# A hybrid decoder layer in split fp32: seven more pairs of matrix blocks by seven products, and split buffers opened and closed in two parts

## The chip, the cores and the metric

The kernel runs on one core of a Trainium2 chip. It is fp32 throughout and its matrix products run on TensorE (PE); VectorE (DVE), ScalarE (ACT) and GpSimd (POOL) do the rest, and SyncE (SP) issues the loads of the weights. Each engine works through its own instructions in a fixed order and waits for the others by semaphores. The time is that of one execution on the device in microseconds, given as the median of several; less is better.

## What is computed

256 tokens of width 2048 go through one layer:

```python
u = rmsnorm(h, ln1_w)
lru_x, lru_g, q, k, v, ret_g = split(u @ w_in)          # 2048 -> 6 x 1024
y_lru = rg_lru(causal_conv4(lru_x)) * gelu(lru_g)
y_ret = group_norm(retention(rope(q), rope(k), v)) * silu(ret_g)
h = h + concat(y_lru, y_ret) @ w_out                    # 2048 -> 2048
u = rmsnorm(h, ln2_w)
h = h + (silu(u @ w_gate) * (u @ w_up)) @ w_down        # 2048 -> 5632 -> 2048
out = rmsnorm(h, final_norm_w)
```

All weights come from HBM once, some 240 MB. The change is in the part from `w_out` on.

## The kernel before

**Splitting.** A matrix product of fp32 accuracy is made of three TensorE products of rounded operands (type fp32r): each operand is split into a high part, the rounded copy, and a low part, the rest. The function `split` (L122) does it: ACT casts (L123: `wh`, `ah`, `sh`, `t4h`, `bh`) and DVE subtracts (L124: `wl`, `al`, `sl`, `t4l`, `bl`). `three` (L680) issues the three matmuls of 128x512: high by high (L683), low weight part (L684), low activation part (L685).

**Pairs and blocks.** From the output projection on, the work is cut into blocks, and a block into pairs: a pair is two 128-row slices of the weights by two 512-column halves, loaded in two transfers of 512 KB (`raw`), and it multiplies the 256 tokens. Blocks 0 and 1 are the output projection, 2 to 12 gate/up (called gate/up 0 to 10 here), each with 8 pairs; then come two down blocks with 22 pairs each. A block sums into four PSUM banks c11, c21, c12, c22. A plain pair takes eight products (24 matmuls; `EIGHT`). A summed pair takes seven (21 matmuls; `SEVEN`), by the Strassen-Winograd scheme: DVE first makes sums of the raw weights (L661, four 512-wide operations a pair) and of the activations (L561 to L564), and these sums are split as well.

**Shared products and the joint.** Of the seven products of a summed pair, four can be done in a block ahead (`Block.share`, L795). They go into the four banks of the coming block while the block before is still at work. When the last of them is done, the banks are rewritten, called the joint here: ACT copies c11 to p1 (L806), DVE makes p = c12 − p1 (L807) and q = p − c22 (L808), ACT copies q to c12 (L809), and DVE makes c22 = q − c21 (L810) and c21 = c21 − p (L811). Only then may the block add its own products to c12, c22 and c21: three for each summed pair (`direct`, L813) and eight for each plain one (`plain`, L817). Down's second block has its summed pairs whole, with no shared part.

**What sets the order.** For each block a string in `STEPS` says what comes after what: `p` a plain pair, `h` half of one, `s` a shared product set for the next block, `d` the direct products of an own summed pair. `SUMMED` lists the summed pairs of each block; for down it is `SUMMED_DOWN` and `ORDER_DOWN`, and `EARLY_DOWN` names the pairs of down's first block that are shared. Loads are issued three ahead of their use. From this program a scheduler makes each engine's order, so that an instruction whose inputs are expected late can move behind others.

**Buffers.** Raw loads have a pool of 6 tiles, splits one of 4 pairs (`wh` and `wl`), the rest 60 activation tiles. From block 3 to block 12 two more raw and two more split buffers are open (`swap` and `stop_more`, L1097 to L1104), in the space that the early stages left. Ahead of down, `swap_back` (L1106) closes them and opens the rows' and weights' pools: the eight kept rows of the residual are loaded back (L1112, POOL's queue) and the four pieces of the final norm's weights `fw` (L893, POOL's queue). In down's second block DVE multiplies finished rows by `fw` (L984).

## Time and profile before

| | before |
|---|---|
| median of 3 runs | 1083.56 us (1082.75 to 1084.05) |
| the profiled execution | 1082.46 us, span 1080.7 us |
| mean granted TensorE clock | 0.998 |
| TensorE busy | 1070.2 us, 99% of the span |
| VectorE busy | 964.1 us, 89% |
| ScalarE busy | 664.5 us, 61% |
| a gate/up block | 41.6 us |

A gate/up block's time is that from one joint to the next between 484.64 and 776.02 us of the span, seven blocks. The span is counted from the first instruction to the last; the execution's own time is a little longer. The chain of waits goes back from the last instruction to what released each; a row of the timeline has its start, its length, engine, line and operation.

### The profile page before, as it was taken

To read this page: it belongs to the slowest core of one execution; us is meant where nothing else is said; L and a number is where in the kernel's file an instruction comes from. 1 tells how busy PE (TensorE), PEld (TensorE's weight loads), DVE (VectorE), ACT (ScalarE), POOL (GpSimd) and SP (SyncE) were. 2 spreads that over 40 slices of the span, in tenths; PEclk is the share of its full clock that TensorE was granted. 3 is DMA by queue.
4 is the path that set the end of the run, shared out by engine and by line. 5 is a ranking of instruction groups with operands and counts; after the bars stand their busy time and mean duration, and the time that the engine had idled before them with its cause. 6 is when DMAs were issued, how large, how long until landed. Compare 5 with 4: busy or idle time off the path is not lost.

```text
span 1080.7 us, 14590 instructions
## 1 busy us (share of the span) xinstructions
PE 1070.2 (99%) x5089; PEld 897.7 (83%) x5089; DVE 964.1 (89%) x1399; ACT 664.5 (61%) x947; POOL 57.2 (5%) x73
## 2 busy tenths in 40 slices
PE   9999999999999999999999999999999999999997
PEld 7888888888888888888888888888888888888886
DVE  7889789988878889989999999999999889997886
ACT  7666644468756676656656565665656656654563
POOL 0602230000000000000000000000002000000001
PEclk9999999999999999999999999999999999999999
DMA  9965475554556588677776777777767856474662
GB/s 325 336 213 171 159 254 166 183 176 158 192 195 234 183 304 273 231 235 256 257 270 228 251 260 242 263 269 232 258 234 270 289 181 214 162 245 159 214 212 101
DMA packets 71386, 244.62 MB, mean 226 GB/s; under 512 B 8208, under 2 KB 8592, under 8 KB 71312
## 3 DMA queue, kind: packets, MB, share of 16 engines
q1 hardware_dynamic: 68400, 236.34, 64.6%
q0 software_dynamic: 1472, 4.72, 1.3%
q10 hardware_dynamic: 1440, 2.62, 0.6%
q8 instruction: 40, 0.66, 0.2%
q14 instruction: 34, 0.28, 0.1%
HBM read 239.46 MB, written 4.19 MB: 225 GB/s over the span
## 4 chain that ended last, share of the span: by engine, by line
PE 98%; DVE 1%; DMA 1%; POOL 0%; SPq 0%; ACT 0%; issue 0%; POOLq 0%; ACTq 0%
PE c L685 22%; PE c L683 22%; PE c L684 22%; PE fm L194 11%; PE fm L196 5%; PE tm L174 3%; PE tm L175 3%; PE tm L176 3%; PE p L683 1%; PE p L685 1%; PE p L684 1%; PE ft L865 1%; DMA x<-in_x 1%; PE ht L588 0%; PE sc L492 0%; DVE wl L124 0%
## 5 line engine op out<-in xcount | busy, mean ns | idle before, releaser
L123 ACT CAST wh<-raw 128x1024 fp32r<-128x1024 f32 (+1 forms) x498 | 462.9, 959 | 323.8 <-PE c L685 130.8
L124 DVE TENSOR_TENSOR wl<-raw,wh 128x1024 fp32r<-128x1024 f32 (+1 forms) x498 | 542.2, 1115 | 72.5 <-ACT wh L123 71.2
L684 PE MATMUL c<-wl,ah 128*128 128x512 f32 x826 | 322.7, 391 | 0.0
L685 PE MATMUL c<-wh,al 128*128 128x512 f32 x826 | 321.8, 390 | 0.0
L683 PE MATMUL c<-wh,ah 128*128 128x512 f32 x826 | 280.3, 391 | 0.0
L683 PEld LDWEIGHTS c<-wh,ah 128*128 128x128 f32 x826 | 155.1, 188 | 32.0 <-ACT wh L123 0.3
L685 PEld LDWEIGHTS c<-wh,al 128*128 128x128 f32 x826 | 155.2, 188 | 31.8
L684 PEld LDWEIGHTS c<-wl,ah 128*128 128x128 f32 x826 | 155.2, 188 | 31.6
L194 PE MATMUL fm<-u,wh 128*128 128x512 f32 x512 | 161.4, 396 | 0.0
L196 PEld LDWEIGHTS fm<-u,wl 128*128 128x128 f32 x512 | 96.1, 188 | 22.4
L196 PE MATMUL fm<-u,wl 128*128 128x256 f32 x512 | 101.2, 279 | 0.0
L661 DVE TENSOR_TENSOR raw<-raw,raw 128x512 f32<-128x512 f32 x114 | 78.4, 689 | 2.0
L661 DVE TENSOR_TENSOR raw<-raw 128x512 f32<-128x512 f32 x114 | 78.3, 688 | 1.4
L194 PEld LDWEIGHTS fm<-u,wh 128*128 128x128 f32 x512 | 78.4, 189 | 0.3
L684 PE MATMUL c<-wl,sh 128*128 128x512 f32 x192 | 74.3, 390 | 0.0
L685 PE MATMUL c<-wh,sl 128*128 128x512 f32 x192 | 73.7, 390 | 0.0
L683 PE MATMUL c<-wh,sh 128*128 128x512 f32 x192 | 67.3, 391 | 0.3 <-ACT sh L123 0.3
L176 PE MATMUL tm<-wh,u 128*128 128x512 f32 x128 | 48.7, 391 | 0.0
L175 PE MATMUL tm<-wl,u 128*128 128x512 f32 x128 | 48.7, 393 | 0.0
L174 PE MATMUL tm<-wh,u 128*128 128x512 f32 x128 | 46.9, 394 | 1.4 <-ACT u L298 1.4
L683 PEld LDWEIGHTS c<-wh,sh 128*128 128x128 f32 x192 | 36.1, 188 | 8.1 <-ACT sh L123 0.7
L685 PEld LDWEIGHTS c<-wh,sl 128*128 128x128 f32 x192 | 36.1, 188 | 7.5
(247 smaller groups left out, 1027.4 us busy)
## 6 DMA issues: line engine op xcount, KB each, us to landing
raw<-in_w_gu SPq DMA_DIRECT2D x216, 512.0 KB, 5.3
raw<-in_w_down SPq DMA_DIRECT2D x91, 512.0 KB, 4.6
raw<-in_w_out SPq DMA_DIRECT2D x34, 512.0 KB, 3.7
raw<-in_w_lx SPq DMA_DIRECT2D x16, 512.0 KB, 6.4
raw<-in_w_k SPq DMA_DIRECT2D x16, 512.0 KB, 3.6
raw<-in_w_q SPq DMA_DIRECT2D x16, 512.0 KB, 4.2
raw<-in_w_rg SPq DMA_DIRECT2D x16, 512.0 KB, 3.5
raw<-in_w_lg SPq DMA_DIRECT2D x16, 512.0 KB, 3.5
```

What stands on the lines that cost most here:

```text
L123: act.copy(out=dst_h, in_=src)
L124: v.tensor_tensor(out=dst_l, in0=src, in1=dst_h.bitcast(F32), op=ALU.subtract)
L174: pe.matmul(ps, ah, wh, start=first, stop=False)
L175: pe.matmul(ps, ah, wl, start=False, stop=False)
L176: pe.matmul(ps, al, wh, start=False, stop=last)
L194: pe.matmul(ps, wh, hl, start=n + i == 0, stop=False)
L196: pe.matmul(ps[:, :S], wl, hl[:, :S], start=False, stop=n + i == len(order) - 1)
L661: v.tensor_tensor(out=dst, in0=a, in1=b, op=ALU.add)
L683: pe.matmul(p, ah, bh, start=first, stop=False, skip_group_check=onto)
L684: pe.matmul(p, ah, bl, start=False, stop=False, skip_group_check=onto)
L685: pe.matmul(p, al, bh, start=False, stop=last, skip_group_check=onto)
L865: pe.transpose(pt[:, o : o + P], g[:, (2 * b + c) * P : (2 * b + c) * P + P], ident)
```

## The change

1. Five more summed pairs in blocks 1, 2, 3 and 12: block 1 goes from two to four, 2 from two to three, 3 and 12 from three to four. The `STEPS` strings of blocks 0 to 3, 11 and 12 change with them; since the strings are given for the coming block's shares, block 0 now has four `s`.
2. Down's second block sums nine pairs and not seven (12 and 19 are new) and takes its pairs in another order.
3. The extra buffers come in two parts. `split_near`, one split buffer, opens already ahead of block 0, and closes in down's second block. `split_far`, one split buffer, and `raw_far`, two raw ones, open ahead of block 3 in the space of the first residual rows and close in down's first block. At these steps (`hooks`) the kept rows come back four by four, and `fw` is loaded when the near part closes, behind step 8 of down's second block. The sums of the activations for pairs 12 and 19 have a pool of their own for a while (`sums`).
4. For the first two column blocks, DVE takes `fw` when the product is run and no longer when it is planned.

The core of the diff:

```diff
-SUMMED = ((), (4, 5), (2, 3), (1, 2, 3)) + ((0, 1, 2, 3),) * 8 + ((1, 2, 3),)
-SUMMED_OUT, SUMMED_FFN = (4, 5), (0, 1, 2, 3)
+SUMMED = ((), (4, 5, 6, 7), (1, 2, 3)) + ((0, 1, 2, 3),) * 10
+SUMMED_OUT, SUMMED_FFN = (4, 5, 6, 7), (0, 1, 2, 3)
...
-STEPS = ("pppspppspp", "ppspdpsdpp", "pdpsdpspspp", "pspsdpsdpsdp") + ("psdhsdhsdhsdhp",) * 7 + ("psdpsdpsddp", "psdpsdpsdpp")
+STEPS = ("ppspspspsppp", "psdpsdpsddp", "pspsdpsdpsdp") + ("psdhsdhsdhsdhp",) * 9 + ("psdpsdpsddp",)
...
-SUMMED_DOWN = (9, 12, 15, 17, 19), (5, 7, 9, 11, 13, 15, 17)
-ORDER_DOWN = (3, 4, 0, 5, 6, 1, 7, 8, 2) + tuple(range(9, 22)), tuple(range(22))
+SUMMED_DOWN = (9, 12, 15, 17, 19), (5, 7, 9, 11, 12, 13, 15, 17, 19)
+ORDER_DOWN = (3, 4, 0, 5, 6, 1, 7, 8, 2) + tuple(range(9, 22)), (0, 12, 1, 19, 2, 5, 3, 7, 4, 9, 6, 11, 8, 13, 10, 15, 14, 17, 16, 18, 20, 21)
+BESIDE = (12, 19)
...
     def split_tiles():
-        turn_of[1] += 1
-        pool_ = more[1] if more and turn_of[1] % 3 == 0 else wpool
-        return [pool_.tile([P, 1024], F32R, tag=g, name=nm(g)) for g in ("wh", "wl")]
+        counts[0] += 1
+        n = counts[0] % (4 + len(more_split))
+        p = more_split[n - 4] if n >= 4 else wpool
+        return [p.tile([P, 1024], F32R, tag=g, name=nm(g)) for g in ("wh", "wl")]
...
+            if i in hooks[ordered]:
+                program.append(([], hooks[ordered][i]))
...
-                defer(13 + 2 * cb + t, lambda: v.tensor_tensor(out=h, in0=h, in1=f, op=ALU.mult))
+                defer(13 + 2 * cb + t, lambda: v.tensor_tensor(out=h, in0=h, in1=fw[cb], op=ALU.mult))
...
+    def near_begins():
+
+        early.close()
+        more_split.append(near.enter_context(tc.tile_pool(name="split_near", bufs=1, reuse_waits="tile")))
...
+    def near_ends():
+        near.close()
+        late.append(ctx.enter_context(tc.tile_pool(name="late", bufs=4, reuse_waits="tile")))
+        load_fw()
+
+    def far_begins():
+
+        kept_stack.close()
+        more_split.append(
+            far.enter_context(tc.tile_pool(name="split_far", bufs=1, side="right", reuse_waits="tile"))
+        )
+        more_raw.append(
+            far.enter_context(tc.tile_pool(name="raw_far", bufs=2, side="right", reuse_waits="tile"))
+        )
...
+    def rows_back(d):
+        resid[0] = ctx.enter_context(tc.tile_pool(name=f"resid_{d}", bufs=4, side="right", reuse_waits="tile"))
+        for key in [(cb, t) for cb in (2 * d, 2 * d + 1) for t in range(2)]:
             htok[key] = res_tile("htok")
             pool.dma_start(out=htok[key], in_=kept[key])
...
+    hooks = {0: {6: far_stops, 9: far_ends}, 1: {5: near_stops, 8: near_ends, 7: sums_end}}
...
     for b, after in zip(blocks, blocks[1:] + [down]):
+        if b.index == 0:
+            program.append(([], near_begins))
         if b.index == 3:
-            program.append(([], swap))
-        if b.index == NB + 1:
-            program.append(([], stop_more))
+            program.append(([], far_begins))
         b.put(after)
-    program.append(([], swap_back))
```

Lines move by three to 29: L123 and L124 become L126 and L127, L661 L664, L683 to L685 L686 to L688, L806 to L811 L811 to L816, L893 L898, L984 L990, L1112 L1141.

**How instructions move, first place: DVE at the joint into gate/up 0.** In the rows c12_777 (before) and c12_793 (after) are banks of gate/up 0; p and q belong to its joint. Before:

```order
L807 TENSOR_TENSOR p_802_3940<-c12_777_3814,p1_801_3939 128x512
L124 TENSOR_TENSOR wl_806_3951<-raw_804_3948,wh_805_3950 128x1024
L124 TENSOR_TENSOR wl_809_3966<-raw_807_3963,wh_808_3965 128x1024
L808 TENSOR_TENSOR q_803_3941<-p_802_3940,c22_775_3806 128x512
L124 TENSOR_TENSOR wl_812_3972<-raw_810_3969,wh_811_3971 128x1024
L810 TENSOR_TENSOR c22_775_3806<-q_803_3941,c21_776_3810 128x512
L811 TENSOR_TENSOR c21_776_3810<-c21_776_3810,p_802_3940 128x512
```

After:

```order
L600 TENSOR_TENSOR htok_629_3132<-c21_679_3364,htok_629_3132 128x512
L127 TENSOR_TENSOR wl_842_4091<-raw_840_4088,wh_841_4090 128x512
L600 TENSOR_TENSOR htok_640_3190<-c12_680_3368,htok_640_3190 128x512
L600 TENSOR_TENSOR htok_652_3251<-c22_678_3360,htok_652_3251 128x512
L664 TENSOR_TENSOR raw_840_4088<-raw_840_4088 128x512
L812 TENSOR_TENSOR p_829_4044<-c12_793_3869,p1_828_4043 128x512
L127 TENSOR_TENSOR wl_836_4070<-raw_834_4067,wh_835_4069 128x1024
L664 TENSOR_TENSOR raw_840_4088<-raw_840_4088,raw_849_4144 128x512
L813 TENSOR_TENSOR q_830_4045<-p_829_4044,c22_791_3861 128x512
L664 TENSOR_TENSOR raw_849_4144<-raw_840_4088,raw_849_4144 128x512
L815 TENSOR_TENSOR c22_791_3861<-q_830_4045,c21_792_3865 128x512
L816 TENSOR_TENSOR c21_792_3865<-c21_792_3865,p_829_4044 128x512
```

Before, the residual rows of the second output block (L597) come behind the joint. Now their four additions (L600 after) stand ahead of it, together with the split wl_842, and two weight sums stand between the steps of the joint. On TensorE, 6 products and 16 transposes of 128x128 now lie between the last shared product of this joint and the first product on c22; before, 50 products.

**Second place: the joint into down's first block**, on TensorE. c12_1666 (before) and c12_1700 (after) are banks of down's first block, c11_1585 to c12_1588 and c22_1612 those of the last gate/up block. Before, the last shared product and its neighbours:

```order
L683 MATMUL c11_1585_7562<-wh_1706_8104,ah_841_4117 128x512
L683 MATMUL c12_1588_7574<-wh_1706_8104,ah_841_4117 128x512
L684 MATMUL c12_1666_7926<-wl_1696_8044,sh_1693_8039 128x512
L685 MATMUL c12_1666_7926<-wh_1695_8043,sl_1694_8040 128x512
L684 MATMUL c11_1585_7562<-wl_1707_8105,ah_841_4117 128x512
L685 MATMUL c11_1585_7562<-wh_1706_8104,al_842_4118 128x512
L684 MATMUL c12_1588_7574<-wl_1707_8105,ah_841_4117 128x512
L685 MATMUL c12_1588_7574<-wh_1706_8104,al_842_4118 128x512
```

After:

```order
L688 MATMUL c22_1698_8025<-wh_1732_8171,sl_1728_8147 128x512
L688 MATMUL c21_1699_8029<-wh_1732_8171,sl_1728_8147 128x512
L688 MATMUL c12_1700_8033<-wh_1729_8150,sl_1728_8147 128x512
L688 MATMUL c22_1612_7639<-wh_1743_8217,al_872_4223 128x512
L686 MATMUL c22_1612_7639<-wh_1749_8244,ah_871_4222 128x512
L687 MATMUL c22_1612_7639<-wl_1750_8245,ah_871_4222 128x512
L688 MATMUL c22_1612_7639<-wh_1749_8244,al_872_4223 128x512
L686 MATMUL c11_1697_8021<-wh_1754_8263,ah_1752_8259 128x512
L686 MATMUL c22_1698_8025<-wh_1754_8263,ah_1752_8259 128x512
L686 MATMUL c21_1699_8029<-wh_1754_8263,ah_1752_8259 128x512
L686 MATMUL c12_1700_8033<-wh_1754_8263,ah_1752_8259 128x512
L687 MATMUL c11_1697_8021<-wl_1755_8264,ah_1752_8259 128x512
```

Before, after the last shared product (the row c12_1666 with sl_1694) 45 products follow up to the first that adds to c12_1666 again. Now four products of the last gate/up block follow the last shared product (c12_1700 with sl_1728), and then down's own products begin on all four banks.

On DVE the same joint, before:

```order
L807 TENSOR_TENSOR p_1712_8127<-c12_1666_7926,p1_1711_8126 128x512
L124 TENSOR_TENSOR wl_1716_8138<-raw_1714_8135,wh_1715_8137 128x1024
L124 TENSOR_TENSOR wl_1719_8153<-raw_1717_8150,wh_1718_8152 128x1024
L808 TENSOR_TENSOR q_1713_8128<-p_1712_8127,c22_1664_7918 128x512
L124 TENSOR_TENSOR al_1722_8159<-ff_1011_4925,ah_1721_8158 128x512
L124 TENSOR_TENSOR wl_1724_8163<-raw_1720_8156,wh_1723_8162 128x1024
L124 TENSOR_TENSOR al_1730_8199<-ff_1090_5291,ah_1729_8198 128x512
L810 TENSOR_TENSOR c22_1664_7918<-q_1713_8128,c21_1665_7922 128x512
L811 TENSOR_TENSOR c21_1665_7922<-c21_1665_7922,p_1712_8127 128x512
```

After:

```order
L812 TENSOR_TENSOR p_1746_8234<-c12_1700_8033,p1_1745_8233 128x512
L813 TENSOR_TENSOR q_1747_8235<-p_1746_8234,c22_1698_8025 128x512
L127 TENSOR_TENSOR wl_1758_8279<-raw_1756_8276,wh_1757_8278 128x1024
L815 TENSOR_TENSOR c22_1698_8025<-q_1747_8235,c21_1699_8029 128x512
L816 TENSOR_TENSOR c21_1699_8029<-c21_1699_8029,p_1746_8234 128x512
L127 TENSOR_TENSOR wl_1755_8264<-raw_1751_8257,wh_1754_8263 128x1024
L127 TENSOR_TENSOR wl_1771_8331<-raw_1769_8328,wh_1770_8330 128x1024
L127 TENSOR_TENSOR al_1753_8260<-ff_1037_4998,ah_1752_8259 128x512
```

p reads the bank of the last shared product. The low part of down's first own activation, al_1753, stands at the end of the queue behind it; before, al_1722 stood ahead of c22.

**Third place: DVE in down's second block**, the products of finished rows with the final norm's weights. Before:

```order
L920 TENSOR_TENSOR htok_1738_8250<-htok_1738_8250,part_1951_9145 128x512
L124 TENSOR_TENSOR wl_1970_9238<-raw_1968_9235,wh_1969_9237 128x1024
L984 TENSOR_TENSOR htok_1735_8244<-htok_1735_8244,fw_1743_8260 128x512
L984 TENSOR_TENSOR htok_1737_8248<-htok_1737_8248,fw_1744_8262 128x512
L941 TENSOR_TENSOR htok_1738_8250<-c22_1664_7918,htok_1738_8250 128x512
L984 TENSOR_TENSOR htok_1736_8246<-htok_1736_8246,fw_1743_8260 128x512
L124 TENSOR_TENSOR wl_1973_9244<-raw_1971_9241,wh_1972_9243 128x1024
L124 TENSOR_TENSOR wl_1980_9278<-raw_1978_9275,wh_1979_9277 128x1024
L984 TENSOR_TENSOR htok_1738_8250<-htok_1738_8250,fw_1744_8262 128x512
```

After:

```order
L127 TENSOR_TENSOR wl_2053_9571<-raw_2047_9556,wh_2052_9570 128x1024
L127 TENSOR_TENSOR wl_2056_9577<-raw_2054_9574,wh_2055_9576 128x1024
L990 TENSOR_TENSOR htok_1855_8715<-htok_1855_8715,fw_2077_9701 128x512
L990 TENSOR_TENSOR htok_1856_8717<-htok_1856_8717,fw_2077_9701 128x512
L990 TENSOR_TENSOR htok_1857_8719<-htok_1857_8719,fw_2078_9703 128x512
L990 TENSOR_TENSOR htok_1858_8721<-htok_1858_8721,fw_2078_9703 128x512
L127 TENSOR_TENSOR wl_2059_9607<-raw_2057_9604,wh_2058_9606 128x1024
L127 TENSOR_TENSOR wl_2069_9652<-raw_2067_9649,wh_2068_9651 128x1024
L127 TENSOR_TENSOR wl_2071_9660<-raw_2060_9610,wh_2070_9659 128x1024
```

The four rows with `fw` stand together now, behind wl_2056 and ahead of wl_2059, and wait for the loads of `fw` that POOL issues when the near split buffer's last reader, a product of the pair before, is done.

53 lines of the change are left out of this document (31 added, 22 removed).

## The prediction

> **What bounds the kernel now.** I read, in this order: the page's busy times and chain, TensorE's waits, the stretches, and then the timelines of VectorE (DVE) and ScalarE (ACT) in one steady block, for the pace of each operation.
>
> ```profile
> PE 1070.2 (99%) x5089; PEld 897.7 (83%) x5089; DVE 964.1 (89%) x1399; ACT 664.5 (61%) x947; POOL 57.2 (5%) x73
> PE 98%; DVE 1%; DMA 1%; POOL 0%; SPq 0%; ACT 0%; issue 0%; POOLq 0%; ACTq 0%
> PE tm L174 <- ACT u L298: 1.4, 2, 1.0
> PE warm L116 <- DVE eps_t L109: 1.1, 1, 1.1
> PE c L683 <- ACT sh L123: 0.3, 1, 0.3
> ```
>
> The chain that ends last is 98% TensorE. Its waits (us in total, times, longest) are three: two at the start, one of 0.3 us in the middle. So the time falls with every matmul that goes, if the operands keep coming, and every new wait of TensorE is added. DVE, at 89%, is the next limit.
>
> ```profile
> 361.71 0.91 PE c L683 x4
> 371.43 0.50 PE c L683
> L685 PE MATMUL c<-wh,al 128*128 128x512 f32 x826 | 321.8, 390 | 0.0
> 344.37 1.64 PE ht L588 x15
> ```
>
> A 512-column matmul takes 0.91/4 = 0.227 us of TensorE; it lasts 390 ns, so its result is seen 0.16 us after its place in the pace. A transpose takes 1.64/15 = 0.11 us.
>
> ```profile
> 616.49 2.47 DVE L124 TENSOR_TENSOR wl<-raw,wh 128x1024 fp32r<-128x1024 f32 x2
> 618.88 0.69 DVE L661 TENSOR_TENSOR raw<-raw,raw 128x512 f32<-128x512 f32 x1
> 629.88 4.09 DVE L124 TENSOR_TENSOR wl<-raw,wh 128x1024 fp32r<-128x1024 f32 x4
> 633.89 0.69 DVE L124 TENSOR_TENSOR t4l<-raw,t4h 128x512 fp32r<-128x512 f32 x1
> 637.96 0.69 DVE L807 TENSOR_TENSOR p<-c,p 128x512 f32<-128x512 f32 x1
> 639.04 1.83 DVE L124 TENSOR_TENSOR wl<-raw,wh 128x1024 fp32r<-128x1024 f32 x2 [0.40 <-ACT wh L123]
> 640.79 0.68 DVE L808 TENSOR_TENSOR q<-p,c 128x512 f32<-128x512 f32 x1
> 641.39 0.68 DVE L661 TENSOR_TENSOR raw<-raw 128x512 f32<-128x512 f32 x1
> 641.99 0.69 DVE L810 TENSOR_TENSOR c<-q,c 128x512 f32<-128x512 f32 x1
> 642.59 0.69 DVE L811 TENSOR_TENSOR c<-c,p 128x512 f32<-128x512 f32 x1
> ```
>
> Each row has its start, its length and the line. From start to start a 512-wide DVE operation takes 0.60 us (641.39, 641.99, 642.59); it lasts 0.69, so 0.09 of it overlaps the next. A 1024-wide one lasts 1231 ns by the group's mean below, so its step is 1.14. The joint of this block (what that is, below) runs here from 637.96 to 643.28, 5.3 us, with two splits and a sum between its steps, and no wait of TensorE follows.
>
> ```profile
> 368.25 0.20 DVE s L562
> L124 DVE TENSOR_TENSOR wl<-raw,wh 128x1024 fp32r<-128x1024 f32 x392 | 476.1, 1231 | 66.1 <-ACT wh L123 64.9
> 587.39 4.42 ACT L123 CAST wh<-raw 128x1024 fp32r<-128x1024 f32 x5 [3.19 <-PE c L685]
> 591.72 0.61 ACT L123 CAST t4h<-raw 128x512 fp32r<-128x512 f32 x1
> 592.24 1.05 ACT L123 CAST wh<-raw 128x1024 fp32r<-128x1024 f32 x1
> 593.19 0.57 ACT L806 COPY p<-c 128x512 f32<-128x512 f32 x1
> 593.66 1.06 ACT L123 CAST wh<-raw 128x1024 fp32r<-128x1024 f32 x1
> ```
>
> The small 128-wide sums take 0.20. On ACT the steps are 0.95 for a 1024 cast (592.24 to 593.19), 0.53 for a 512 cast, 0.47 for the copy (593.19 to 593.66).
>
> **What is removed.** Seven pairs go from 24 matmuls to 21: 21 x 0.227 = 4.76 us of TensorE. The products behind the 0.3 us wait stand elsewhere in the order now, so I let it go too: 5.06 us in all, if TensorE never waits again.
>
> **What is added.** For the seven pairs DVE has 28 more L664 sums (0.60 each, 16.8 us), 10 more 512 splits and some smaller; ACT 21 more casts; SP 5 more 512 KB loads. In the stretches
>
> ```profile
> 360.00:380.00 20.00, 19.70 (x87) 15.82 (x86) 18.66 (x29) 13.56 (x19) 0.00 (x0) 1.00 0.61 199
> 480.00:500.00 20.00, 20.00 (x94) 16.57 (x93) 19.44 (x25) 11.73 (x17) 0.00 (x0) 1.00 0.69 224
> 1060.00:1080.00 20.00, 12.97 (x69) 11.03 (x67) 11.60 (x31) 7.19 (x18) 4.16 (x5) 0.92 0.30 106
> ```
>
> (length, then busy time of PE, PEld, DVE, ACT, POOL, then clock and DMA) DVE is full in a gate/up block (19.44 of 20) but has room in total: 1080 − 964 = 116 us. Added work as such is hidden by TensorE; what counts is where it stands in the in-order queues, above all at a **joint**: when the last shared product of a block is done, DVE must make p, q, c22 and c21 (L812 to L816) and ACT copy q back to c12, before the block's own products add to those banks. I counted TensorE's work between the last shared product and the first product that needs the rewritten bank. Before, c22 had 7.3 us or more and c12 5.4 or more at every joint; the trace shows no wait at any. Now one has almost none, one has half, and three are close. "Due" below is when TensorE would want the product if nothing were late, 0 the end of the last shared product.
>
> **E, joint into down's first block.** Before, 45 products of the last gate/up block (10.2 us) stood behind the last shared product. Now 4 do (c22_1612). DVE's queue: p 0.2 to 0.8 (0.16 us until the product is seen), q 1.4, wl_1758 2.54, c22 3.14, c21 3.74, wl_1755 4.88, wl_1771 6.02, al_1753 6.62, seen at 6.7. al_1753 is due after 4 + 8 products, 12 x 0.227 = 2.72. So 4.0 us late. On ACT casts wh_1757, wh_1754, wh_1770, ah_1752 end at 3.3, against 0.9 due: the same wait begins there, 2.4 us of it in one piece. Nothing else of TensorE lies between. **4.0.**
>
> **A, second output block and joint into the first gate/up block.** First: c12_680<-wh_820 is directly followed by c11_677<-wh_823, and the cast wh_823 waits for just that product's buffer: 0.16 + 0.95 + 0.1 = 1.2 us. Then the joint (c12_793): cover for c22 is 6 products and 16 transposes, 3.1 us. DVE can't begin wl_824 before that cast, and from wl_824 to p its queue is 5 x 1.14 + 11 x 0.60 + 4 x 0.20 = 13.1 us, while TensorE takes 12.0 from its c11_677 to the last shared product: p starts 0.16 + 0.9 after it. Then p, wl_836, a sum, q, a sum, c22, 5 x 0.60 + 1.14 = 4.1: c22 is seen at 5.3, due at 3.1, 2.2 more. **3.4**; 2.5 with no queue ahead of p (1.2 + 4.4 − 3.1), 6 if a load is late besides. The 512 KB loads land 5.3 us after issue,
>
> ```profile
> raw<-in_w_gu SPq DMA_DIRECT2D x216, 512.0 KB, 5.3
> ```
>
> so one that is issued too late costs some 3 us more, which makes the 6.
>
> **B, C, D, joints into gate/up blocks 3, 9 and 10.** The cover of c12 is 4.8, 5.2 and 3.9 us. D worked out: p 0.2 to 0.8, two 1024 splits to 3.1, q 3.7, a 512 split 4.3, wl_1665 5.4; due 4.1, with ACT's copy at 4.2 against 3.9: 1.4. The same sum gives 1.5 at B and 0.8 at C. These queues begin with p, which waits for TensorE itself, so casts that run ahead would not shorten them. **3.7 together**, 0 if the steps are shorter than I read, 5 with 0.4 more each.
>
> **F, final-norm weights.** They were loaded once, 150 us ahead of use; now POOL loads them when the near split buffer is released, 48 products (10.9 us) before TensorE needs wl_2059, which stands behind the four L990 rows in DVE.
>
> ```profile
> L893 POOL DMA_DIRECT2D fw<-in_final_norm_w x4: 536/537/577, 811.2 to 812.9; - x4
> L984 DVE TENSOR_TENSOR htok<-htok,fw x4: 681/685/686, 962.0 to 966.7; 128x512 f32<-128x512 f32 x4
> DMA to landing us min/median/max: 3.4/5.8/6.5
> ```
>
> Each row of fw has the issue's length (536 ns) and, last, the time from issue to landing. 0.16 + 0.54 + (3.4 to 6.5) + 4 x 0.60 + 1.14 = 7.6 to 10.7 us, just inside 10.9; the splits behind (wl_2073, wl_2076) come out 0 to 0.7 late. **0.7**; nothing if the loads are quick, 4.7 more if they take as long as the slowest of the htok rows' transfers:
>
> ```profile
> DMA to landing us min/median/max: 2.3/5.4/11.2
> ```
>
> The other edits (the sums' own pool, kept rows back in two parts, a split buffer more from block 0) go at nothing: they move waits for buffers, and the casts behind them stand in ACT's queue, idle 39% of the span. Without that cover each late cast would be a 1.2 as at A. They could gain as well: before, no wait for a buffer shows in TensorE's waits but the 0.3, so at most that.
>
> **The sum.** The same adding-up on the kernel before gives one late place, in the second output block, by 0.76 us, where the trace has 0.30. I take the difference, 0.46, as an error of the method, and the smaller half of it, 0.3, off each of the six places, since the chains here are shorter: 4.0 + 3.4 + 3.7 + 0.7 = 11.8, less 6 x 0.3 is 10.0. Net 10.0 − 5.06 = +4.9. The profiled execution took 1082.46 us and would take 1087.4; the median of the runs, 1083.56, lies 1.1 above it: **1088.5**.
>
> **Rivals.**
> 1. *All hidden.* The joints cost nothing, as none did before: the products that wait are few, and TensorE would lose nothing if DVE stood ready at E. It would take c22 within 1.1 us of the last shared product, where three 512-wide steps alone are 1.8. 1083.56 − 5.06 = 1078.5. Chance 0.07.
> 2. *The queues at the joints run shorter than read.* If the method overstates by a ratio and not by an amount, they are 11.8 x 0.30/0.76 = 4.7, E is 1.6, and saving and waits cancel: 1083.56 − 5.06 + 4.7 = 1083.2. For it: the one place where both are known. Against: p, q and c22 in a row give E 0.16 + 1.8 + 0.09 − 0.9 = 1.1 before any split or cast is counted. It decides from an E under 2.5. Chance 0.17.
> 3. *The late weights.* From a landing of 6.7 us on (10.9 less the 4.2 of the other terms) every microsecond is TensorE's. With 11.2, and A at its 6: 4.0 + 6 + 3.7 + 0.7 + 4.7 − 1.8 − 5.06 = +12.2, 1095.8. For it: one queue for the reloads and the weights. Against: POOL had landed all four within 6.5. Chance 0.13.
> 4. *The clock falls in the waits.* The one stretch with long idle, the last (12.97 busy of 20), ran at 0.92: 12.97 x 0.08 = 1.0 us. At A and E together that gives 1090.5. Against: the stretch with the 0.3 us wait is at 1.00, and the longest single piece I find is 2.4 us. Chance 0.05.
>
> [...]
>
> That the pairs are not made of seven products is excluded: the changed program has 21 fewer matmuls of 512 columns.
>
> **Chances and range.** The forecast holds 0.58, with its own range of 1085.8 to 1092. A measurement of this kernel can tell about 0.2%, 2.2 us: 1081.4 to 1085.7 is no change, and that is rival 2. Faster 0.08, same 0.17, slower 0.75. The range goes from rival 2 to near rival 3: 1083.0 to 1095.0.
>
> **What would show it.** In the changed profile TensorE's busy time should be 4.8 us less, and its waits should hold some 10 us: about 3.7 at the start of down's first block (c L686 and L688 behind ACT ah and DVE al), 3 around the first gate/up block's beginning, 1 at each of three joints, and 0 to 1 behind the four L990 rows. If the wait at E is under 2 us, DVE's queue there isn't what I read. If the waits are as said and the span is still not longer, the pace is not what sets it. If new waits name a raw's DMA, the loads are the matter, which I gave little.

## The result, and the profile after

| | before | changed |
|---|---|---|
| median of 4 runs each, same chip | 1083.62 us (1082.75 to 1084.05) | 1101.65 us (1099.75 to 1104.54) |
| ratio | | 1.017, interval 1.0146 to 1.0193 |
| span of the profiled execution | 1080.7 us | 1099.3 us |
| mean granted TensorE clock | 0.998 | 0.994 |

The changed kernel is slower, as forecast, but by 18.0 us and not by 4.9; the time lies above the range. The first and the fourth part of its page, busy times and the chain of waits:

```profile
PE 1079.0 (98%) x5068; PEld 894.3 (81%) x5068; DVE 993.8 (90%) x1456; ACT 675.7 (61%) x968; POOL 57.4 (5%) x73
PE 87%; DVE 4%; DMA 3%; ACT 2%; issue 2%; POOL 1%; SPq 0%; POOLq 0%; ACTq 0%; DVEq 0%
```

There are 21 matmuls fewer (5068 for 5089), and yet TensorE is busy for 8.8 us more. Of the chain 87% is TensorE now, before it was 98%: DVE, DMA and ACT have come in. TensorE's waits (us in total, times, longest):

```profile
PE c L686 <- ACT ah L126: 2.7, 2, 2.4
PE c L687 <- DVE wl L127: 2.5, 3, 1.2
PE c L686 <- ACT c L814: 2.3, 2, 1.7
PE c L686 <- ACT wh L126: 1.7, 4, 1.1
PE c L686 <- DVE c L815: 1.0, 1, 1.0
```

These five rows hold 10.2 us and the forecast had 10.0. The agreement is luck in part: A came out larger than forecast, E smaller, and nothing came at F (below). Most of the miss lies where no wait is listed. Three stretches show two further things; the columns are the stretch, its length, the busy time (and count) of PE, PEld, DVE, ACT and POOL, the granted clock, the DMA share and GB/s. The changed kernel, then the one before:

```profile
380.00:400.00 20.00, 17.68 (x77) 13.94 (x76) 18.06 (x29) 15.53 (x27) 0.00 (x0) 0.91 0.84 283
460.00:480.00 20.00, 20.00 (x89) 16.36 (x88) 19.36 (x25) 11.33 (x14) 0.00 (x0) 1.00 0.85 284
860.00:880.00 20.00, 17.61 (x74) 13.63 (x73) 15.63 (x21) 11.89 (x16) 0.00 (x0) 0.91 0.76 251
```

```profile
380.00:400.00 20.00, 20.00 (x98) 16.67 (x97) 16.77 (x28) 16.47 (x31) 0.00 (x0) 1.00 0.89 323
460.00:480.00 20.00, 20.00 (x90) 16.58 (x89) 17.30 (x24) 13.24 (x17) 0.00 (x0) 1.00 0.77 256
860.00:880.00 20.00, 20.00 (x90) 16.55 (x89) 18.02 (x33) 13.62 (x18) 0.00 (x0) 1.00 0.58 187
```

**The clock.** In the first and the third stretch it is 0.91: for 3.41 us in each it ran at half speed (0.50 from 394.07 and from 865.11 us). The chain at down's first joint (E) shows it: start, length, what.

```profile
862.25 0.70 DVE p L812
...
864.72 0.24 DVE c L815
864.96 0.53 ACT ah L126
...
865.53 2.23 PE c L686 x4
867.76 1.33 PE c L687 x4
869.09 1.02 PE c L688 x4
```

p, c22 and the cast `ah` come one behind the other, as the forecast had them for E; TensorE stands from 862.98 to 865.53, 2.56 us. Four products then take 2.23 us, where 0.91 is their time at full speed. At E this costs 1.5 us beside the waits, at A (394.1 to 397.5) 1.6. This is the profiled execution. A piece of 3.41 us at half clock takes 0.5 x 3.41 / 1099.3 = 0.0016 off the mean clock, and the four executions of the changed kernel had 0.994, 0.996, 0.996 and 0.994, so by this estimate two of them had fewer such pieces.

**The pace.** The second stretch has no wait and a clock of 1.00, and still one product fewer than before. In its chain:

```profile
462.06 0.94 PE c L686 x4
469.68 1.16 PE c L686 x5
```

That is 0.235 and 0.232 us a product; before, it was 0.91/4 = 0.227. The slow ones are those whose weights lie in `split_far`, the far split buffer: 0.2336 us on the mean from block 3 on, and more than nine in ten of them are slow. Of the other products from 400 us on nearly a quarter took 0.230 us or more as well, against 2% before.

**Where the 18.6 us of span come from.** I add up, over the whole trace, what lies between the start of one product and the next beyond the product's own pace:

| | us |
|---|---|
| 21 products fewer | −4.8 |
| waits of over 0.3 us: A 4.7, B 1.6, C 0.8, D 1.8, E 2.9, F 1.1 | +12.9 |
| half clock at A and E | +3.1 |
| slower pace | about +5.5 |
| the rest, in pieces under 0.3 (the first product after a wait takes 0.34, not 0.23) | +1.9 |

The pace stands as 5.5 since the small pieces from 400 us on sum to 6.3, and to 0.8 in the experiment that restores it. The waits are 2.7 more than the rows above, since those count from the end of the product before, which lasts 0.16 beyond its place.

**A** is larger than forecast. Its chain, and the first steps of F's below it:

```profile
375.35 4.25 DMA raw<-in_w_out
...
379.70 1.06 ACT wh L126
...
380.78 2.36 DVE wl L127 x2
...
389.68 0.60 DVE p L812
390.28 1.13 DVE wl L127
...
392.01 0.60 DVE q L813
...
393.21 0.61 DVE c L815
```

```profile
1027.94 5.39 DMA raw<-in_w_down
...
1033.35 0.63 ACT bh L126
```

At A the load of a raw tile, issued when DVE let its buffer go at 375.35, lands at 379.6; from then on DVE works through its queue with hardly a break to c22 at 393.8. At F the three small waits of the table stand at 1025.9, 1036.9 and 1047.6, well behind the rows with `fw`; the chain through them goes back over three raw loads, of which the first is shown, and not to `fw`. The view of the tile `fw` (shortest, median and longest duration, first and last start; the time from issue to landing):

```profile
L898 POOL DMA_DIRECT2D fw<-in_final_norm_w x4: 536/536/538, 1010.4 to 1012.0; - x4
L990 DVE TENSOR_TENSOR htok<-htok,fw x4: 684/688/693, 1015.8 to 1017.6; 128x512 f32<-128x512 f32 x4
DMA to landing us min/median/max: 5.4/5.6/5.8
```

The four rows L990 ran as soon as `fw` was there, and no wait of TensorE stands behind them.

### The profile page after: what moved, and what is told of

Same layout as the page of the kernel before. It is cut to its first block, busy times and chain, and to the rows that moved or that the text cites. A ratio compares the mean times of both kernels' runs of the same rounds, so it can differ in the third digit from the quotient of the medians.

```text
span 1099.3 us, 14639 instructions
## 1 busy us (share of the span) xinstructions
PE 1079.0 (98%) x5068; PEld 894.3 (81%) x5068; DVE 993.8 (90%) x1456; ACT 675.7 (61%) x968; POOL 57.4 (5%) x73
## 4 chain that ended last, share of the span: by engine, by line
PE 87%; DVE 4%; DMA 3%; ACT 2%; issue 2%; POOL 1%; SPq 0%; POOLq 0%; ACTq 0%; DVEq 0%
PE c L686 20%; PE c L687 20%; PE c L688 20%; PE fm L197 10%; PE fm L199 5%; PE tm L178 2%; PE tm L177 2%; PE tm L179 2%; DVE wl L127 2%; DMA raw<-in_w_down 1%; ACT wh L126 1%; PE p L686 1%; PE p L687 1%; PE ft L870 1%; PE p L688 1%
## 5 line engine op out<-in xcount | busy, mean ns | idle before, releaser
L126 ACT CAST wh<-raw 128x1024 fp32r<-128x1024 f32 (+1 forms) x510 | 468.1, 952 | 302.7 <-PE c L688 106.5
L127 DVE TENSOR_TENSOR wl<-raw,wh 128x1024 fp32r<-128x1024 f32 (+1 forms) x510 | 550.0, 1105 | 58.8 <-ACT wh L126 57.7
L687 PE MATMUL c<-wl,ah 128*128 128x512 f32 x784 | 307.6, 394 | 2.5 <-DVE wl L127 2.5
L688 PE MATMUL c<-wh,al 128*128 128x512 f32 x784 | 304.3, 392 | 0.0
L686 PE MATMUL c<-wh,ah 128*128 128x512 f32 x784 | 274.1, 396 | 7.8 <-ACT ah L126 2.7
L686 PEld LDWEIGHTS c<-wh,ah 128*128 128x128 f32 x784 | 147.8, 189 | 43.4 <-ACT wh L126 3.7
L688 PEld LDWEIGHTS c<-wh,al 128*128 128x128 f32 x784 | 147.6, 188 | 31.7 <-DVE al L127 0.3
L664 DVE TENSOR_TENSOR raw<-raw,raw 128x512 f32<-128x512 f32 x128 | 87.9, 687 | 1.9
L664 DVE TENSOR_TENSOR raw<-raw 128x512 f32<-128x512 f32 x128 | 87.3, 686 | 1.3
L687 PE MATMUL c<-wl,sh 128*128 128x512 f32 x214 | 83.2, 392 | 0.0
L688 PE MATMUL c<-wh,sl 128*128 128x512 f32 x214 | 82.3, 391 | 0.0
L686 PE MATMUL c<-wh,sh 128*128 128x512 f32 x214 | 75.6, 394 | 0.0
L688 PEld LDWEIGHTS c<-wh,sl 128*128 128x128 f32 x214 | 40.2, 188 | 8.8
L687 PEld LDWEIGHTS c<-wl,sh 128*128 128x128 f32 x214 | 40.2, 188 | 8.7
```

The source lines that it names most:

```text
L126: act.copy(out=dst_h, in_=src)
L127: v.tensor_tensor(out=dst_l, in0=src, in1=dst_h.bitcast(F32), op=ALU.subtract)
L664: v.tensor_tensor(out=dst, in0=a, in1=b, op=ALU.add)
L686: pe.matmul(p, ah, bh, start=first, stop=False, skip_group_check=onto)
L687: pe.matmul(p, ah, bl, start=False, stop=False, skip_group_check=onto)
L688: pe.matmul(p, al, bh, start=False, stop=last, skip_group_check=onto)
```

## The experiments

For each run I also give the time TensorE lost: what the products' starts fall behind the sum of their paces, from 340 us on to the last product. Waits, half clock and slow pace are all in it. "Saved" is the products' time that the run has less than before. Lost time and half-clock pieces are those of the profiled execution alone, and the pieces differ between executions of one kernel: the mean clock of e1 was 0.995 in the profiled one and 0.997 to 0.998 in the three others. In the quoted expectations "the first run" is e1, "the fourth" e4, and so on; the turn of the split buffers is the order in which they are taken.

| run | median us | ratio, interval | lost | saved | pieces of 3.41 us at half clock |
|---|---|---|---|---|---|
| before | 1083 | 1 | 1.3 | 0 | none |
| the change | 1101.65 | 1.017, 1.0146 to 1.0193 | 24.8 | 4.8 | 2 |
| e1 32 bytes ahead of the far buffers | 1100.56 | 1.0162, 1.014 to 1.0183 | 26.8 | 4.8 | 2 |
| e2 before, extra buffers moved by 32 bytes | 1088.67 | 1.0056, 1.0039 to 1.0072 | 7.4 | 0 | none |
| e3 e1, another order in the last gate/up block | 1098.28 | 1.0142, 1.0127 to 1.0158 | 21.8 | 4.8 | none |
| e4 new buffers, old pairs, 32 bytes ahead | 1104.08 | 1.0192, 1.0176 to 1.0208 | 24.0 | 0 | 4 |
| e5 96 bytes ahead of the far buffers | 1099.58 | 1.0148, 1.0135 to 1.0161 | 22.8 | 4.8 | 3 |
| e6 old buffers, five new pairs | 1100.55 | 1.0159, 1.0146 to 1.0172 | 22.2 | 3.4 | 3 |
| e7 old buffers, four new pairs | 1092.78 | 1.0082, 1.007 to 1.0094 | 14.7 | 2.7 | 3 |
| e8 e9 with the old turn of the split buffers | 1086.69 | 1.003, 1.002 to 1.004 | 4.8 | 0 | none |
| e9 e4 at multiples of 128 | 1101.24 | 1.0165, 1.0149 to 1.018 | 22.7 | 0 | 4 |
| e10 old buffers, one new pair | 1084.25 | 1.0013, 1.0004 to 1.0022 | 3.7 | 0.7 | none |
| e11 e5 with the old turn | 1105.73 | 1.0203, 1.018 to 1.0226 | 26.9 | 4.8 | 4 |
| e12 e8 with down's nine pairs | 1092.98 | 1.0085, 1.0064 to 1.0106 | 15.9 | 1.4 | 1 |

Each ratio is against the kernel before on the same chip in the same session, whose medians there were 1082.94 to 1083.17.

### The addresses: e1, e2, e5

In the built program every raw, split and activation buffer of the kernel before starts at a multiple of 128 bytes; in the changed one the far buffers lie on the right side of the memory, 96 bytes beyond one (221152, say). The first theory put the slow pace down to that. e1 puts 32 bytes ahead of them, so that they lie 64 beyond a multiple of 128:

```diff
+    pad = ctx.enter_context(tc.tile_pool(name="pad", bufs=1, side="right"))
+    v0pad = pad.tile([P, 8], F32, name="pad8")
+    nc.vector.memset(v0pad, 0.0)
```

> The changed kernel with an unused 32-byte tile at the outer end of the right side, so that the residual rows, split_far, raw_far and the sums' pool lie at multiples of 64 bytes and not 32 beside them; every engine's order is as before. Theory (address): from 400 us on the matmuls whose weights lie in split_far took 0.2336 us and not 0.2267, and some of their neighbours too, 6.3 us in sum; this goes, so about 1095.5. Rival (traffic): the far part or the extra DVE work slows the matmuls wherever it lies; then 1101 to 1102 and the pace stays.

The pace stayed slow, 0.232 to 0.233 us for weights in the far buffer, so at 64 bytes beyond a multiple of 128 too. (The pad also exchanges a few rows of DVE and ACT in the early stages; TensorE's order, and all orders from the output projection on, are the same.) That left open whether addresses matter at all. e2 asks it in the kernel before, with nothing else changed: the two extra raw and split buffers are moved up by 32 bytes.

```diff
+        pad = extra.enter_context(tc.tile_pool(name="pad", bufs=1))
+        v.memset(pad.tile([P, 8], F32, name="pad8"), 0.0)
```

> The kernel before, with a 32-byte tile ahead of the two extra raw and two extra split buffers, which so lie 32 bytes beside multiples of 64; orders unchanged. Theory (address): a third of the split buffers are now slow to read from block 3 to block 12, so 4 to 9 us longer, 1088 to 1093, with matmuls of 0.233 us. Rival (traffic): no change, 1083 to 1084.

It cost 5.6 us, with TensorE's one wait of 0.3 us from 340 us on as before and no piece at half clock. The chain of a steady block in e2, then in the kernel before:

```profile
620.32 0.93 PE c L683 x4
```

```profile
617.75 0.91 PE c L683 x4
```

So the place of these buffers alone slows the products, from 0.227 to 0.232 or 0.233. e5 puts the changed kernel's buffers at multiples of 128, with 96 bytes:

```diff
-    v0pad = pad.tile([P, 8], F32, name="pad8")
+    v0pad = pad.tile([P, 24], F32, name="pad24")
```

> The changed kernel with an unused 96-byte tile at the outer end of the right side: its buffers now lie at multiples of 128 bytes as all buffers of the kernel before do (in the first run they lay 64 beside). Orders unchanged. Theory (address, with 128 as the step): the slow matmuls (0.232 to 0.236 us) go, the small excess over 0.2267 falls from 6 to 7 us to about 0.5, and the time is 6 less: 1094 to 1096. Rival (it is the far part's use and not its address): the pace stays and the time is 1100 to 1102.

The pace came back: 0.2268 us for weights in the far buffer, and the small pieces fell from 6.3 to 0.8 us. The span fell by 2.2 us only, and the median by 2.1, with intervals that overlap; 6 had been forecast. Two of its stretches:

```profile
460.00:480.00 20.00, 20.00 (x90) 16.57 (x89) 19.58 (x26) 12.04 (x16) 0.00 (x0) 1.00 0.85 290
520.00:540.00 20.00, 18.45 (x77) 14.53 (x76) 18.36 (x25) 11.60 (x17) 0.00 (x0) 0.91 0.66 225
```

In the first there are 90 products again, as before. In the second, at B, there is one more piece at half clock, which the changed kernel (clock 1.00 in that stretch) did not have. A faster TensorE comes to the next joint earlier, and DVE is no faster: I read it so that part of what the pace gave back was waited away there. B's waits are 0.95 and 0.94 us, 0.70 and 0.93 in the changed kernel.

### The joint into down: e3

E's cover was worked out from the order alone: four products between the last shared one and the first that needs the cast. e3 is e1 with the end of the last gate/up block in another order, so that more own products stand behind the last shared one.

```diff
-STEPS = (...) + ("psdhsdhsdhsdhp",) * 9 + ("psdpsdpsddp",)
+STEPS = (...) + ("psdhsdhsdhsdhp",) * 9 + ("psdpsdsdpdp",)
```

> The changed kernel, aligned as in the first run, with the last gate/up block's steps psdpsdsdpdp in place of psdpsdpsddp: the last shared product of down's first block comes with 7.7 us of other products before c22 is needed, not 1.1. Theory (joint): the 3.0 us of waits at the start of down's first block and the half-clock stretch behind them, about 1.5, go: 4.5 less than the first run, some 1091. Rival (the wait moves): the splits are late anyhow and the wait shows at the next product, so within 1.5 of the first run.

In e1 TensorE waited 2.56 + 0.58 + 0.36 us at E. In e3 it has no wait at that joint (p at 857.4, c21 done at 863.3), and the piece at half clock is gone:

```profile
860.00:880.00 20.00, 20.00 (x93) 16.55 (x92) 16.36 (x22) 12.63 (x18) 0.00 (x0) 1.00 0.72 239
```

In their place stand two waits, of 1.49 and 0.87 us in the measure of the table, some 8 to 12 us ahead of that joint, behind a cast and a split of weights:

```profile
847.08 1.20 PE L689 MATMUL c<-wh,ah 128*128 128x512 f32 x4 [1.32 <-ACT wh L129]
850.26 0.50 PE L690 MATMUL c<-wl,ah 128*128 128x512 f32 x1 [0.70 <-DVE wl L130]
```

The median fell by 2.3 us against e1, where 4.5 had been forecast, and the two intervals overlap. So the order around the last shared product makes the wait at E, as the forecast had it, but with the new order DVE and ACT come late earlier in the same block, and 2.4 of the 3.5 us are lost there. The waits at B, C and D stayed. The piece at half clock at A, which the edit does not touch, is gone as well: A's waits are nearly the same, so I take it for a difference between executions (see the clock, below).

### The buffers alone: e4, e9, e8

The forecast gave "the other edits" nothing. e4 has them alone: the changed kernel (with e1's 32 bytes) and the pairs, orders and steps of the kernel before.

```diff
-SUMMED = ((), (4, 5, 6, 7), (1, 2, 3)) + ((0, 1, 2, 3),) * 10
+SUMMED = ((), (4, 5), (2, 3), (1, 2, 3)) + ((0, 1, 2, 3),) * 8 + ((1, 2, 3),)
...
-BESIDE = (12, 19)
+BESIDE = ()
```

> The changed buffers alone, aligned, with the pairs, steps and orders of the kernel before (no pair more by seven products). Theory (the waits come from the added pairs and their steps): within 1 of before, 1083 to 1084.5. Rival (the buffers' turn itself shortens what lies between a joint and its readers, since the order made from it has 4.1 us there at down's first block and 3.9 at one gate/up block): 1 to 4 us slower than before, 1085 to 1088.

It is as slow as the whole change, with no pair added, far beyond both forecasts. e9 is e4 at multiples of 128 bytes (the edit of e5), to take the pace out:

> The fourth run (the changed buffers, the pairs and steps of before) with its right side at multiples of 128 bytes; the order is the same, row for row. It stands between the fourth and the eighth run, which differed in address and in the turn of the split buffers. Theory (address and turn are separate): the pace comes back, 5.5 us, the waits at the same places stay (450, 600 to 750, at down's first block, and in its second), so 1097 to 1100, less or more by the half-clock stretches of 1.7 us each; the eighth run's further gain of 10 is the turn's. Rival (the address makes the waits too): near the eighth run, 1087 to 1090.

Full pace, and 2.8 us came back where 5.5 had been forecast; 22.7 us are still lost, in waits at 643, 731, 772, 855 to 861 and 1010 to 1017 us and four pieces of 3.41 us at half clock, 1.7 us of TensorE's work each. At 772 us, what ACT and DVE were held by:

```profile
765.65 0.62 ACT L129 CAST wh<-raw 128x512 fp32r<-128x512 f32 x1 [3.66 <-DMA raw<-in_w_gu]
766.31 0.69 DVE L130 TENSOR_TENSOR wl<-raw,wh 128x512 fp32r<-128x512 f32 x1 [1.98 <-ACT wh L129]
```

A raw load came late, ACT stood 3.66 us for it and DVE 1.98 for ACT, just ahead of a joint; DVE had then two splits between p and q, and TensorE waited 2.58 for a `wl`. e8 keeps e9's buffers and takes them in turn as the kernel before did: every third split goes to an extra buffer, near and far alternating, and none does while only the near one is open.

```diff
-        n = counts[0] % (4 + len(more_split))
-        p = more_split[n - 4] if n >= 4 else wpool
+        p = more_split[counts[0] // 3 % 2] if len(more_split) > 1 and counts[0] % 3 == 0 else wpool
```

> The fourth run again (the changed buffers, the pairs and steps of before) with two things as in the kernel before: addresses at multiples of 128 bytes, and the turn of the split buffers (every third one from the two extra, from block 3 on). They are still open into the down blocks, and the rows and final-norm weights come back late. Theory (the buffers' turn costs the waits at the joints): the waits of gate/up and of down's first block fall from 9 us to under 4, the pace is full, so about 1088 to 1091. Rival (the late end of the buffers in down costs it): the waits behind 1010 us stay and gate/up's too, over 1094.

1086.69: that line by itself is worth 14.5 us against e9, with the same buffers open and the same pairs. It does two things. It changes the turn while both extra buffers are open; but there both turns hand each of the six buffers out once in six splits. And it leaves the near buffer unused while the far one is closed, in blocks 0 to 2 and from step 6 of down's first block on; e9 uses it from block 0 into down's second block. No run separates the two. What else the changed buffers have, later rows and `fw` included, is all in e8, which is 3.5 us above the kernel before. What moved from e9 to e8 is the order that the scheduler makes: in gate/up and at the joint into down, the rows in DVE's queue from p to c22 are at most 6 in e8, and up to 10 in e9; and the shortest cover of c12's copy behind the last shared product is 4.3 us in e8, 3.9 in e9, that of c22 5.9 and 4.1. e9's waits in gate/up lie at the joints with the short cover or the long queue, though one joint with ten rows (809 us) has no wait. That is read from the orders and not tried: why this line gives the better order, I can't say.

### The pairs alone: e6, e7, e10, e12

e6 is the kernel before with the five new pairs of blocks 1, 2, 3 and 12 and their steps; buffers and down stay.

```diff
-SUMMED = ((), (4, 5), (2, 3), (1, 2, 3)) + ((0, 1, 2, 3),) * 8 + ((1, 2, 3),)
+SUMMED = ((), (4, 5, 6, 7), (1, 2, 3)) + ((0, 1, 2, 3),) * 10
...
-STEPS = ("pppspppspp", "ppspdpsdpp", "pdpsdpspspp", "pspsdpsdpsdp") + ("psdhsdhsdhsdhp",) * 7 + ("psdpsdpsddp", "psdpsdpsdpp")
+STEPS = ("ppspspspsppp", "psdpsdpsddp", "pspsdpsdpsdp") + ("psdhsdhsdhsdhp",) * 9 + ("psdpsdpsddp",)
```

> The kernel before with its own buffers, but the changed table of summed pairs and steps for the output and gate/up blocks (five more pairs, 15 matmuls less; down as before). Its order has 5.5 us or more between the joints and c12 everywhere but at one gate/up block (c22 2.0 us, c12 3.6). Theory (the waits come from what the changed buffers make of the order): 3.4 less for the matmuls, 2 to 3 back at that joint, so 1082 to 1083.5, with TensorE at full pace. Rival (the added pairs themselves overload VectorE): waits at most joints, 1086 to 1092.

Full pace, and 22.2 us lost, far beyond both forecasts: at 362 to 375 us, 3.75 at 400, at the joints at 530 and 863, with half clock three times. So the joints' waits come without the new buffers too. e7 takes four pairs, with steps that leave more cover at every joint (8.2 us for c22 and 6.3 for c12 at least, where the kernel before has 7.3 and 5.4):

```diff
+SUMMED = ((), (4, 5, 6, 7), (2, 3)) + ((0, 1, 2, 3),) * 10
+STEPS = ("ppspspspsppp", "pdsdpdsdpp", "pspdspspdspp") + ("psdhsdhsdhsdhp",) * 9 + ("psdpsdpsddp",)
```

> The kernel before with its own buffers and four pairs more by seven products (two in the second output block, one in the second gate/up block, one in the last), with steps chosen so that the order has at least 8.2 us between each joint and c22 and 6.3 to c12. Theory: no wait at any joint, 12 matmuls less, 2.7 us faster than before: 1080 to 1081. Rival (VectorE's added sums show up as waits): 1083 or more.

Better than e6 by 7.8 us and still slower than before. The chain at its last joint:

```profile
847.01 2.37 DVE wl L124 x2
849.39 6.66 DMA raw<-in_w_down
...
856.15 1.06 ACT wh L123
857.23 1.07 DVE wl L124
...
858.37 0.70 DVE al L124
859.11 0.50 PE c L685
```

Cover at the joint is not enough: DVE's splits let a raw buffer go late, the load takes 6.66 us, the cast and the split follow, and TensorE waits at the end. At 365 to 372 us the chain is nearly all DVE. e10 adds a single pair, in gate/up 1:

```diff
-SUMMED = ((), (4, 5), (2, 3), (1, 2, 3)) + ((0, 1, 2, 3),) * 8 + ((1, 2, 3),)
+SUMMED = ((), (4, 5), (2, 3)) + ((0, 1, 2, 3),) * 9 + ((1, 2, 3),)
-STEPS = ("pppspppspp", "ppspdpsdpp", "pdpsdpspspp", "pspsdpsdpsdp") + ("psdhsdhsdhsdhp",) * 7 + ("psdpsdpsddp", "psdpsdpsdpp")
+STEPS = ("pppspppspp", "ppspdpsdpp", "pspdspspdspp") + ("psdhsdhsdhsdhp",) * 8 + ("psdpsdpsddp", "psdpsdpsdpp")
```

> The kernel before with its own buffers and one pair more by seven products, in the second gate/up block (block 3), whose steps and one neighbour's change; its order keeps 8.2 us or more to c22 at every joint. Theory (a pair costs nothing where the order keeps joints and loads ahead): 0.7 us less, 1082 to 1083.3, no wait of TensorE over 0.5. Rival (any new order brings waits): 1085 or more.

0.7 us saved, 2.4 more lost. The median, 1084.25, lies between the two forecasts, 1.1 us above the kernel before, whose own executions in that session lay 2.0 us apart. The wait at 404 us goes back to one load:

```profile
394.53 8.47 DMA raw<-in_w_gu
```

e12 adds to e8 what the change does in down's second block, nine pairs, the new order and the sums' own pool:

```diff
-SUMMED_DOWN = (9, 12, 15, 17, 19), (5, 7, 9, 11, 13, 15, 17)
+SUMMED_DOWN = (9, 12, 15, 17, 19), (5, 7, 9, 11, 12, 13, 15, 17, 19)
...
-BESIDE = ()
+BESIDE = (12, 19)
```

> The eighth run (changed buffers at multiples of 128 bytes, the turn and the pairs of before) with the change in down's second block alone: nine summed pairs in their new order, 6 matmuls less. Theory (the added pairs bring waits where they stand): 1.4 less for the matmuls, 4 to 7 more in waits behind VectorE between 925 and 1010 us, 1090 to 1093. Rival (those pairs are covered): 1085 to 1086.

6.3 us slower than e8, with 1.4 saved, as forecast. The waits and the chain of that block:

```profile
PE p L688 <- ACT bh L128: 4.0, 3, 2.3
PE p L688 <- ACT wh L128: 2.6, 4, 0.8
```

```profile
974.13 7.04 DMA raw<-in_w_down
...
987.77 8.27 DMA raw<-in_w_down
996.06 0.63 ACT bh L128
```

Again loads that are asked for late, when DVE has let a buffer go, and take 7 to 8 us. These nine pairs don't cost that much with any buffers: e5 has them too and uses the near buffer in the first of that part, and loses 3.5 us there, where e12 loses 11.7 (the table further below).

### The old turn with all the pairs: e11

If the turn was the cause of the change's loss, then e5 with e8's line should come near the kernel before.

> The changed kernel with all its pairs, at multiples of 128 bytes (the fifth run) and with the split buffers' turn of the kernel before (as in the eighth run). Theory (the turn costs the waits): some 10 less than the fifth run, 1088 to 1091. Rival (the added pairs in the second output block cost as much with any buffers, as in the sixth and seventh run): the order has 2.7 us to c22 at down's first joint and long queues of VectorE between 340 and 390 us, so 1098 to 1106.

It did not: 1105.73, slower than e5. With the pairs in, the waits only lie at other places (361 to 369, 3.76 us at 400, 852 to 867, 980 to 983), and they sum to more, as the rival had it. But e8's line also keeps the near buffer from the second output block, where two of the new pairs are: up to some 410 us TensorE's order is that of e6, row for row, and the largest waits are e6's (2.4 us at 362, 3.75 at 400). So e11 does not try the old turn with the buffers of the change in use.

## Why the prediction was right, and where it was not

**The saving** of 4.76 us came: there are 21 products of 0.227 us fewer. That TensorE's busy row would fall by 4.8 was wrong: it rose by 8.8, since slow products, and the 0.16 us that the product ahead of each wait lasts beyond its place, count as busy.

**The waits at the joints** were there, at the places named. E: 4.0 forecast, 2.9 measured; the one piece of 2.4 behind ACT's casts came as 2.56, and of the 1.6 behind DVE's `al` only 0.3 shows. I take it that the other 1.3 lie in the half clock, which held TensorE back there by 1.5 anyway; no run shows the one without the other. B 1.5 and 1.6, C 0.8 and 0.8, D 1.4 and 1.8. A: 3.4 forecast, 4.7 measured; its first part, c11_677 behind the cast wh_823, was put at 1.2 and took 1.3, the rest 3.4 for 2.2. The term that was too small is DVE's start: a raw load that landed at 379.6 put its whole queue back, which the prediction had as the case of 6 ("if a load is late besides") and not as its own. F: 0.7 forecast, and nothing came there: `fw` landed 5.4 to 5.8 us after issue and held nobody. The 1.1 us booked as F stand further on in the block and go back to raw loads, so that this term comes near is luck. The 0.3 that I took off each place made the sum worse: 11.8 is nearer to the 12.9 than 10.0. So a joint's wait can be read from the order and the paces to some 0.4 us at B, C and D, where nothing comes in from outside, and not where a load stands ahead.

**The rivals.** All hidden (1) and shorter queues (2) fall: E is over the 2.5 from which the second would decide. The late weights (3) fall with `fw`'s 5.8 us at most. The clock (4) came in, on top of more waits than forecast.

**What failed**, in the order of size:

1. "The other edits ... go at nothing." The reason given was that they move waits for buffers, behind which ACT's idle 39% stands. It takes the pace of 0.227 us as given for every product; the new addresses of the buffers changed it, which cost about 5.5 us of the changed kernel (e2, e5). The order that came with the buffers was no term left out, as the queues at the joints were read from the changed order. But the waits there were put down to the added pairs, and the buffers alone, with the old pairs, lose as much (e4, e9), where the kernel before had no wait but the 0.3.
2. "The clock falls in the waits. Chance 0.05", priced 1.0 a place. It happened at A and E, at 1.6 and 1.5 us. The price was read from the stretch 1060 to 1080 us, where the half clock begins only at 1076.7, behind the last product. That the longest single piece found was 2.4 us was a wrong reason against it: at E the half clock came behind 2.56 us in one piece, and at A behind two pieces of 1.40 and 1.15.
3. The waits, 12.9 us for 10.0: the 0.3 taken off each of six places (1.8), and A's late load (1.3), with small differences at the others. A raw buffer is let go by DVE's last split or sum of it, so a DVE that is late makes the load late, which then takes 4.25 us (A) to 8.47 us (e10), and the cast and the split behind it. In the prediction that chain stands once, as A's upper bound. It is what most experiments end in (A and F here, e7, e9, e10, e12).
4. The range. It ended at 1095.0, below the 1095.8 of the prediction's own third rival, and held nothing for item 1.

With items 1 and 2 and the waits as measured, the forecast would have been 1088.5 + 5.5 + 3.1 + 2.9 = 1100.0; 1.6 of the 1101.65 are the small rest.

**The effects don't add up.** The buffers alone come to 1101.24 us at full pace (e9), the first five pairs alone to 1100.55 (e6), both together to 1099.58 (e5, with down's pairs too). Nor does a loss that is taken away come back whole: e5 took away 5.5 and gained 2.1. Cut by place, the lost time (us, worked out as in the table of runs, with sums within 0.2 of it) shows more; the edges lie 2 us ahead of the joint into gate/up 1, 12 behind the one into gate/up 10, and 15 behind the one into down:

| run | up to gate/up 0 | gate/up 1 to 10 | joint into down | the rest |
|---|---|---|---|---|
| before | 0.9 | 0.4 | 0.1 | 0.1 |
| e9 buffers alone | 0.1 | 9.0 | 6.6 | 7.1 |
| e6 five pairs alone | 11.3 | 5.8 | 4.3 | 1.0 |
| e5 both, and down's pairs | 7.0 | 7.2 | 5.2 | 3.5 |
| e8 e9 with e8's line | 1.6 | 3.2 | 0.1 | 0.1 |
| e12 e8 with down's pairs | 0.9 | 3.3 | 0.1 | 11.7 |
| e11 e5 with e8's line | 14.2 | 2.9 | 3.5 | 6.5 |

The pairs lose most around the second output block, where the buffers alone lose nothing; the buffers alone lose from gate/up 1 on. With both, no place loses more than the worse of the two does alone. So no single part is the cause of the slowdown, and either suffices; I take it that each of the two takes DVE, busy for 87% of the span in e4 and 90% in e6, and the loads that wait for it, out of step. The first two theories of the experiments (the addresses, the turn) each hold for their part and fail for the whole.

**What stays open.** Why e8's line makes the better order. With the new pairs, too, it gives 4.3 us in gate/up 1 to 10 and 1.7 at the joint into down (e11 against e5); it takes 7.2 around the second output block and 3.0 at the end, where it leaves the near buffer unused and new pairs stand. The old turn together with the near buffer in use there was not tried. The orders differ in cover and queue at the joints as said, but no run changes those alone. Whether the pairs can be had with steps that keep DVE up was tried in e7 and e10 only; neither of them, nor any other version, was faster than the kernel before.

## What to carry to other kernels

A kernel whose bound engine never waits, with the next one at 90%, has an order that is worth more than a few saved products (here 24.8 us lost for 4.8 saved): before a change, follow for each joint the whole loop of buffer, load, cast and split, and not the joint's own queue alone. When buffers move, compare their addresses with the old ones: here 32, 64 or 96 bytes beyond a multiple of 128 went with 0.232 to 0.235 us a product in place of 0.227. Where waits are forecast, add up those that lie close together and not gap by gap: at A the half clock came behind two pieces of 1.40 and 1.15 us. Two executions can differ: those of the changed kernel had mean clocks of 0.994 and 0.996.

## What was not expected of the hardware

**Addresses.** Measured in these runs, by the place of the buffer that a 512-column fp32r product streams its weights from: 0.232 to 0.233 us a product at 32 bytes beyond a multiple of 128 (e2) and at 64 (e1), 0.232 to 0.235 at 96 (the changed kernel), 0.227 at multiples of 128 (the kernel before, e5). Nothing in a list of waits shows it, and no run shows the reason.

**The clock.** In the changed kernel's trace the granted clock is 0.50 from 394.07 and from 865.11 us, each time for 3.413 us, and from 1093.81 us to the end, behind the last product; elsewhere it is 1.00. The three starts lie 471.04 and 228.69 us apart, 138.0 and 67.0 times 3.413. Idle is counted here as in the tables, each product for its full-speed pace. If the trace is cut into stretches of 3.413 us with edges at these starts, the two stretches just ahead of the drops at A and E have 2.08 and 2.17 us idle, and no other one from 340 us on to the last product has more than 1.94. That is one trace; in e6 2.13 us went by without a drop, so no bound is shown. One pair has the same gap and both clocks. The same wait, behind 16 transposes, in e6 and then in e11 (start, length, instruction, idle before and its releaser):

```profile
398.98 1.91 PE L588 MATMUL ht<-ident,htok 128*128 128x128 f32 x16
404.48 0.50 PE L683 MATMUL c<-wh,ah 128*128 128x512 f32 x1 [3.59 <-ACT hf L591]
404.82 0.40 PE L684 MATMUL c<-wl,ah 128*128 128x512 f32 x1
```

```profile
397.94 1.91 PE L593 MATMUL ht<-ident,htok 128*128 128x128 f32 x16
403.44 0.79 PE L688 MATMUL c<-wh,ah 128*128 128x512 f32 x1 [3.59 <-ACT hf L596]
404.03 0.63 PE L689 MATMUL c<-wl,ah 128*128 128x512 f32 x1
```

The wait is 3.59 in both. In e6 the products behind it last 0.40 us, and the clock from 395 to 415 us is 1.00; in e11 they last 0.63, up to 406.2, and the clock of the same stretch is 0.91. In e6 an earlier piece at half clock begins at 365.3; stretches of 3.413 us counted on from there have an edge near 402.9, in the wait, and the two beside it have 2.13 and 1.77 us idle in all. In e11 the piece at half clock begins near 402.9, and the stretch just ahead of it has 3.16. So in these three traces the half clock came behind stretches of 2.08, 2.17 and 3.16 us idle and not behind 2.13 and 1.77, and behind a single gap of 2.56 us at E and not behind 3.59 in e6. No run changes either alone, and what sets the clock is not shown.
